# Both products of each attention score on a full 128-row operand: the low half of k stacked twice, in both layers

## The chip, the cores and the metric

The kernel runs on one core of one Trainium2 chip. The metric is device time in microseconds (us) of one execution, taken as the median of several. TensorE (PE) does the matrix products, VectorE (DVE) and ScalarE (ACT) the elementwise work, GpSimd (POOL) some elementwise work and the issue of one DMA queue, SyncE (SP) the issue of another.

## The reference

A two-layer backbone over 256 context and 512 latent tokens (768 in all, width 1024). Layer 0 mixes with differential attention beside a gated delta rule, layer 1 with a bidirectional linear recurrence (RG-LRU) beside windowed attention; a gated convolutional feed-forward follows each. The change touches only the scores of the two attentions:

```
def _diff_attend(q, k, v, lam):                 # layer 0: 4 heads, 2 maps m, 64 wide
    s = jnp.einsum('bqhmd,bkhmd->bhmqk', q, k).astype(jnp.float32) * (A_HD ** -0.5)
    p = jax.nn.softmax(s, axis=-1)
    w = p[:, :, 0] - lam * p[:, :, 1]
    return jnp.einsum('bhqk,bkhe->bqhe', w.astype(v.dtype), v)
...
    def attend(q, k, v, mask):                  # layer 1: 8 query heads on 2 k/v heads, 64 wide
        s = jnp.einsum('bqhgd,bkhd->bhgqk', q, k).astype(jnp.float32) * (D_HD ** -0.5)
        if mask is not None:
            s = jnp.where(mask, s, NEG_INF)
        p = _sink_softmax(s, sink)
        return jnp.einsum('bhgqk,bkhd->bqhgd', p.astype(v.dtype), v)
```

## The kernel before

Products that must be as good as float32 are made of a high and a low part of each operand: hi is the rounded value, lo what is left. A score is q_hi k_hi + q_lo k_hi + q_hi k_lo. Heads are 64 wide, and the operands lie with the head's 64 numbers over the partitions, so the first two terms fit into one 128-row product: one operand tile holds q_hi in one half of the 128 partitions and q_lo in the other, and the k tile holds k_hi twice. The third term is a second product with 64 rows only: the half of the q tile that holds q_hi, and the matching half of a tile with k_lo.

**Layer 0, `attn_head` (L596 on).** Heads run one after the other. For each there are three groups of query tiles of 128 queries: tiles 2 and 3 and tiles 4 and 5 against all 768 keys, tiles 0 and 1 against the 256 context keys. Per query tile and map m a score of 128 queries is written to a PSUM buffer `sc` (three buffers), in pieces of 512 and 256 key columns; each piece is the 128-row product at L613 and then the 64-row product at L614. A pair of the two stands below as "a pair": there are 20 in each head, 8 with 512 columns and 12 with 256, so 80 in all. VectorE then takes the row maximum (`reduce_max`, L615, `st`), ScalarE the exponential (L617, `e`, five buffers), VectorE normalises the two maps and subtracts them (L619 to L621), PE transposes the result (L626) and multiplies it with v (L631, `pav`). Gate projections (plain 128-row products, L341 to L344) are placed behind heads 0 and 1. The order of all instructions comes from a scheduler in the framework that builds the program, not from the code's order alone.

`attn_load` (L953 on) fetches the q and k tiles of a head from DRAM on POOL's DMA queue (L962): five tiles of tag `qk` per head by nine DMAs, four pairs of 64-row DMAs and a 128-row one (both maps' k_lo, one after the other). The tag has `NQK` = 7 buffers, so two tiles of the next head can be loaded while all five of a head are in use.

**Layer 1, `swa_block` (L1220 on).** 32 blocks (4 query tiles, 2 k/v heads, 4 query heads each): two 128-row products (L1237, the context columns and the window), two 64-row products (L1239), masks added by a bf16 product (L1242), then maximum, exponential (L1248), transposes (L1255) and the product with v (L1260). The layer's `sc` has one PSUM buffer. `halves` (L931) splits k into `k1` (k_hi in one half of the rows, copied to the other half by a POOL DMA, one tile per k/v head) and `k1l` (k_lo of head 0 in rows 0 to 63 and of head 1 in rows 64 to 127, one tile). These tiles come from a ring of `SLOTS` = 22 slots shared with the recurrence (`lt`, `gx`, `la`); `SL1` = 16 is the size of another pool, with the 16 tiles of the layer's normalised input.

Of the kernel before, what the change touches and what calls it, by code (L numbers as in the profile page):

```python
# [9 lines left out]
F32 = mybir.dt.float32  # L10
F32R = mybir.dt.float32r
BF16 = mybir.dt.bfloat16
AF = mybir.ActivationFunctionType
ALU = mybir.AluOpType
# [4 lines left out]
P = 128  # L19
# [223 lines left out]
class K:  # L243
# [213 lines left out]
        nc.vector.scalar_tensor_tensor(q, x, 0.0, q, op0=ALU.max, op1=ALU.add)  # L457
        return q

# [1 line left out]
    def ada_init(self):  # L461
        nc = self.nc
        self.sv = self.small(16, "sv")
# [79 lines left out]
            B.append(self.mod[l][s][:, 8 * m:8 * (m + 1)])  # L543
        return A, B

# [1 line left out]
    def loadx(self, pool=None, eng=None):  # L547
        xs = []
        for kt in range(KT):
# [46 lines left out]
    def attn_head(self, h, qk, Vh, o, pool, ae):  # L596
        nc = self.nc
        ident = self.c("ident")
        for (t0, nt, k1) in ((2, 2, T), (4, 2, T), (0, 2, NC)):
            nkt = k1 // P  # L600
            wts = [pool.tile([P, 3, 256], F32, tag="wT", name=self.nm("wT"), bufs=NWT) for _ in range((nkt + 2) // 3)]
            for qi in range(nt):
                qt = t0 + qi
                es = []
                st = pool.tile([P, 6], F32, tag="st", name=self.nm("st"), bufs=8)
                for m in range(2):
                    ps = self.big("sc")
                    q, k, kl = qk[3 * m], qk[3 * m + 1], qk[2]
                    lq = q[:, qt * P:qt * P + P]
                    half = slice(64 * m, 64 * m + 64)  # L610
                    for a in range(0, k1, 512):
                        b = min(a + 512, k1)
                        nc.tensor.matmul(ps[:, a:b], lq, k[:, a:b], start=True, stop=False)  # L613
                        nc.tensor.matmul(ps[:, a:b], lq[half], kl[half, a:b], start=False, stop=True)  # L614
                    nc.vector.reduce_max(st[:, m:m + 1], ps[:, 0:k1], axis=AX.X, negate=True)  # L615
                    e = ae.tile([P, T], F32, tag="e", name=self.nm("e"), bufs=NE)
                    nc.scalar.activation(e[:, 0:k1], ps[:, 0:k1], AF.Exp, bias=st[:, m:m + 1], accum_out=st[:, 2 + m:3 + m])  # L617
                    es.append(e)
                nc.vector.reciprocal(st[:, 4:6], st[:, 2:4])  # L619
                nc.vector.tensor_scalar(es[1][:, 0:k1], es[1][:, 0:k1], st[:, 5:6], self.nlam, op0=ALU.mult, op1=ALU.mult)  # L620
                nc.vector.scalar_tensor_tensor(es[0][:, 0:k1], es[0][:, 0:k1], st[:, 4:5], es[1][:, 0:k1], op0=ALU.mult, op1=ALU.add)  # L621
                for g in range(0, nkt, 3):
                    gn = min(3, nkt - g)
                    pt = self.sml("pT")
                    for j in range(gn):
                        nc.tensor.transpose(pt[:, j * P:j * P + P], es[0][:, (g + j) * P:(g + j + 1) * P], ident)  # L626
                    nc.scalar.activation(wts[g // 3][:, 0:gn, qi * P:qi * P + P],
                                         pt[:, 0:gn * P].rearrange("p (a b) -> p a b", a=gn), AF.Copy)
            po = self.sml("pav")
            for kt in range(nkt):  # L630
                nc.tensor.matmul(po[:, 0:nt * P], Vh[:, kt * P:kt * P + P], wts[kt // 3][:, kt % 3, 0:nt * P],  # L631
                                 start=kt == 0, stop=kt == nkt - 1)
            nc.scalar.activation(o[:, t0 * P:(t0 + nt) * P], po[:, 0:nt * P], AF.Copy)
# [297 lines left out]
    def halves(self, x, st, l, moves):  # L931
        nc = self.nc
        rows = (slice(0, 64), slice(64, P))
        for i, (me, other) in enumerate((rows, rows[::-1])):
            nc.scalar.activation(st[i][me], x[me], AF.Copy)
            HE[i](nc).tensor_tensor(l[me], x[me], st[i][me].bitcast(F32), op=ALU.subtract)
            dst, src = moves[i]
            HQ(nc).dma_start(dst[other], src[me])

# [13 lines left out]
    def attn_load(self, h, at):  # L953
# [1 line left out]
        up, dn = slice(0, 64), slice(64, P)  # L955
        q, k = self.qdr[h], self.qdr[4 + h]
        r = []
        for src in (((q, 0, up), (q, 1, up)), ((k, 0, up), (k, 0, up)), ((k, 1, slice(0, P)),),
                    ((q, 1, dn), (q, 0, dn)), ((k, 0, dn), (k, 0, dn))):
            t = at.tile([P, T], F32R, tag="qk", name=self.nm("qk"), bufs=NQK)  # L960
            for o, (d, i, rows) in zip((up, dn) if len(src) > 1 else (slice(0, P),), src):
                nc.gpsimd.dma_start(t[o], d[i, rows])  # L962
            r.append(t)
        return r

    def attn_v(self, h, u):
# [253 lines left out]
    def swa_block(self, i, qs, kk, V):  # L1220
# [7 lines left out]
        for kv in range(2):  # L1228
            ks = slice(64 * kv, 64 * kv + 64)
            pT = [lp.tile([P, 512], F32, tag="pT1", name=self.nm("pT1"), bufs=7) for _ in range(nkt)]  # L1230
            for g in range(4):
# [4 lines left out]
                for o, a, b in cols:  # L1236
                    nc.tensor.matmul(ps[:, o:o + b - a], lq, kst[kv][:, a:b], start=True, stop=False)  # L1237
                for o, a, b in cols:
                    nc.tensor.matmul(ps[:, o:o + b - a], lq[ks], kl[ks, a:b], start=False, stop=o == 256)  # L1239
                ms = [j for j in range(lo, hi) if j != i]  # L1240
                for j in ms:
                    nc.tensor.matmul(ps[:, 512 + (j - lo) * P:512 + (j - lo + 1) * P], self.mk[:, 0, :],  # L1242
# [29 lines left out]
    def layer1_body(self, xs, r):  # L1272
# [4 lines left out]
        with tc.tile_pool(name="l1", bufs=1, reuse_waits="tile") as lp:  # L1277
# [7 lines left out]
            kk = self.slot([P, T], F32, "kk")  # L1285
            nc.scalar.activation(kk, ps[:, 256:1024], AF.Copy)
            self.rope(kk, self.slot([P, NL], F32, "rt"), eng=RE[0] and nc.vector)
            kst, kl = [self.slot([P, T], F32R, "k1") for i in range(2)], self.slot([P, T], F32R, "k1l")
            self.halves(kk, kst, kl, [(kst[0], kst[0]), (kst[1], kst[1])])
            ps = psv  # L1290
            vT = self.slot([P, T], F32, "vT")
            nc.scalar.activation(vT, ps[:, 256:1024], AF.Copy)
# [56 lines left out]
AD1 = 7  # L1349
OH = 0  # L1350
GATES = ((0, 1), (2, 3), (), ())
NQK = 7
NE = 5
NWT = 3
ADS = 2
# [11 lines left out]
PSML = 1  # L1367
LOPOOL = 3
SFF = 7
SL1 = 16  # L1370
NY = 4
WRAW = 3
WHL = 4
# [21 lines left out]
```

## Time and profile before

| what | value |
|---|---|
| runs (us) | 2015.21, 2019.02, 2019.27; median 2019.02 |
| profiled execution | span 2016.1 us from its first to its last instruction; no other time of it is given |
| mean granted TensorE clock | 0.933 |
| PE busy | 1881.8 us, 93% of the span |
| DVE busy | 1281.7 us, 64% |
| ACT busy | 902.6 us, 45% |
| POOL busy | 498.7 us, 25% |

"Granted clock" is the share of full TensorE speed that the chip allowed: 1.00 is 2.4 GHz, 0.50 is 1.2 GHz. Layer 0's attention lies between 507 and 685 us of the span, layer 1's windowed attention between 1393 and 1572 us. In a timeline row the first number is the start, the second the time until the instruction's end; successive matmuls overlap (the next one's columns enter while the last one's results drain), so the cost of one in a row of matmuls is the distance between starts, not the second number.

### The profile page before, as it was taken

To read this page: it belongs to the slowest core of one execution; us is meant where nothing else is said; L and a number is where in the kernel's file an instruction comes from. 1 tells how busy PE (TensorE), PEld (TensorE's weight loads), DVE (VectorE), ACT (ScalarE), POOL (GpSimd) and SP (SyncE) were. 2 spreads that over 40 slices of the span, in tenths; PEclk is the share of its full clock that TensorE was granted. 3 is DMA by queue.
4 is the path that set the end of the run, shared out by engine and by line. 5 is a ranking of instruction groups with operands and counts; after the bars stand their busy time and mean duration, and the time that the engine had idled before them with its cause. 6 is when DMAs were issued, how large, how long until landed. Compare 5 with 4: busy or idle time off the path is not lost. (4 is left out here: it accounts for less than half of the span.)

```text
span 2016.1 us, 26630 instructions
## 1 busy us (share of the span) xinstructions
PE 1881.8 (93%) x9929; PEld 1509.7 (75%) x9929; DVE 1281.7 (64%) x2364; ACT 902.6 (45%) x1638; POOL 498.7 (25%) x352
## 2 busy tenths in 40 slices
PE   7687889899999999999999999979999999999997
PEld 2576778778666688888888888867555688888887
DVE  5987888775446556665755454576666685555556
ACT  4355533342556455432334232365566464333344
POOL 1546322212121024312323122132121331111112
PEclk9799988788788799999999999989999999999998
DMA  8434222222321133323344334233000232333324
GB/s 313 147 105 146 79 91 91 92 69 69 68 60 45 53 125 126 117 91 114 129 129 138 113 123 136 82 96 92 27 21 21 68 126 89 111 94 95 94 79 121
DMA packets 74801, 200.86 MB, mean 100 GB/s; under 512 B 8320, under 2 KB 18736, under 8 KB 74288
## 3 DMA queue, kind: packets, MB, share of 16 engines
q1 hardware_dynamic: 65984, 173.01, 26.6%
q10 hardware_dynamic: 4752, 16.85, 2.5%
q0 software_dynamic: 3936, 9.31, 2.2%
q8 instruction: 78, 1.28, 0.2%
q14 instruction: 51, 0.42, 0.1%
HBM read 187.71 MB, written 9.99 MB: 98 GB/s over the span
## 5 line engine op out<-in xcount | busy, mean ns | idle before, releaser
L328 ACT ACTIVATE hi<-raw 128x512 fp32r<-128x512 f32 (+2 forms) x429 | 262.0, 616 | 447.1 <-PE pj L342 197.5
L341 PE MATMUL pj<-uh,hi 128*128 128x512 f32 x1248 | 441.1, 353 | 16.1 <-DVE cv L433 13.0
L342 PE MATMUL pj<-ul,hi 128*128 128x512 f32 x1248 | 413.8, 351 | 0.0
L330 POOL TENSOR_TENSOR lo<-raw,hi 128x512 fp32r<-128x512 f32 (+1 forms) x143 | 194.2, 1358 | 791.0 <-ACT hi L328 783.2
L344 PE MATMUL pj<-uh,lo 128*128 128x512 f32 x1248 | 347.1, 353 | 0.0
L330 DVE TENSOR_TENSOR lo<-raw,hi 128x512 fp32r<-128x512 f32 (+2 forms) x286 | 207.0, 727 | 158.0 <-ACT hi L328 156.5
L341 PEld LDWEIGHTS pj<-uh,hi 128*128 128x128 f32 x1248 | 242.7, 194 | 73.1 <-issue 11.1
L342 PEld LDWEIGHTS pj<-ul,hi 128*128 128x128 f32 x1248 | 242.4, 194 | 28.7 <-issue 0.2
L344 PEld LDWEIGHTS pj<-uh,lo 128*128 128x128 f32 x1248 | 203.0, 196 | 4.4 <-issue 0.8
L433 DVE SCALAR_TENSOR_TENSOR y<-pj,smt,y 128x511 f32<-128x511 f32 (+1 forms) x264 | 161.6, 655 | 57.8 <-ACT y L423 55.2
L341 PE MATMUL dn<-h,hi 128*128 128x512 f32 (+1 forms) x560 | 194.9, 348 | 1.5 <-ACT hi L328 1.0
L342 PE MATMUL dn<-l,hi 128*128 128x512 f32 (+1 forms) x560 | 186.9, 346 | 0.0
L344 PE MATMUL dn<-h,lo 128*128 128x512 f32 (+1 forms) x560 | 169.4, 347 | 1.9 <-DVE lo L330 1.3
L558 DVE SCALAR_TENSOR_TENSOR x<-dn,mod,x 128x512 f32<-128x512 f32 (+1 forms) x152 | 93.2, 634 | 90.6 <-PE dn L344 90.4
L518 ACT ACTIVATE srow<-srow 128x1024 f32<-128x1024 f32 x56 | 59.3, 1058 | 159.9 <-POOL srow L517 159.8
L341 PE MATMUL pj<-u,hi 128*128 128x512 f32 x336 | 130.7, 389 | 0.0
L342 PE MATMUL pj<-u,hi 128*128 128x512 f32 x336 | 130.7, 389 | 0.0
L344 PE MATMUL pj<-u,lo 128*128 128x512 f32 x336 | 130.7, 389 | 0.0
L341 PEld LDWEIGHTS dn<-h,hi 128*128 128x128 f32 x560 | 106.0, 189 | 22.9 <-ACT hi L328 2.2
L517 POOL TENSOR_TENSOR srow<-ada1w,srow 128x1024 f32<-128x1024 f32 x32 | 79.6, 2487 | 173.0 <-DMA ada1w<-in_ada 128.5
L342 PEld LDWEIGHTS dn<-l,hi 128*128 128x128 f32 x560 | 106.2, 190 | 13.7 <-issue 0.5
L523 DVE SCALAR_TENSOR_TENSOR ada1w<-ada1w,srow 128x1024 f32<-128x1024 f32 x40 | 54.6, 1365 | 76.8 <-DMA ada1w<-in_ada 36.4
(394 smaller groups left out, 3406.6 us busy)
## 6 DMA issues: line engine op xcount, KB each, us to landing
raw<-in_wu SPq DMA_DIRECT2D x88, 512.0 KB, 3.5
ada1w<-in_ada SPq DMA_DIRECT2D x48, 512.0 KB, 3.6
raw<-in_w SPq DMA_DIRECT2D x38, 512.0 KB, 3.7
raw<-in_wd SPq DMA_DIRECT2D x72, 256.0 KB, 2.7
adaw<-in_ada0t ACTq DMA_DIRECT2D x24, 512.0 KB, 3.6
adaw<-in_ada SPq DMA_DIRECT2D x16, 512.0 KB, 7.4
raw<-in_w0o SPq DMA_DIRECT2D x16, 512.0 KB, 3.5
raw<-in_wd SPq DMA_DIRECT2D x40, 192.0 KB, 2.4
```

What stands on the lines that cost most here:

```text
L328: nc.scalar.activation(hi, raw[:, a:b], AF.Copy)
L330: eng.tensor_tensor(lo, raw[:, a:b], hi.bitcast(F32), op=ALU.subtract)
L341: nc.tensor.matmul(ps, hi[n], xh[:, a:b], start=n == 0, stop=False)
L342: nc.tensor.matmul(ps, hi[n], xl[:, a:b], start=False, stop=False)
L344: nc.tensor.matmul(ps, lo[n], xh[:, a:b], start=False, stop=n == last)
L433: nc.vector.scalar_tensor_tensor(y[:, o0:o1], ps[:, 256 + o0 + s:256 + o1 + s], taps[i], y[:, o0:o1], op0=ALU.mult, op1=ALU.add)
L517: nc.gpsimd.tensor_tensor(junk, raw, self.srow[:, 0, :], op=ALU.mult)
L518: nc.scalar.activation(junk, junk, AF.Copy, accum_out=col(0))
L523: nc.vector.scalar_tensor_tensor(raw, raw, 1.0, self.srow[:, i, :], op0=ALU.mult, op1=ALU.mult, accum_out=col(i))
L558: nc.vector.scalar_tensor_tensor(xs[m][:, a:b], ps[:, 256 + a:256 + b], self.mod[l][0 if a >= NC else 1][:, 8 * mi + m:8 * mi + m + 1], xs ...
```

## The change

The low half of k is stacked twice over the partitions as the high half was, so that the second product of each score also takes the full 128-row q tile. It computes (q_hi + q_lo) k_lo where q_hi k_lo was computed. In layer 0 each map gets a k_lo tile of its own: six tiles per head by twelve 64-row DMAs, and `NQK` is 8. In layer 1 there are two `k1l` tiles, each filled to 128 rows by one more POOL DMA, and `SL1` is 17. Two comments fall away, so lines 610 to 935 are one lower in the changed kernel. The numbers of matmuls, of VectorE and of ScalarE instructions do not change.

```diff
@@ -605,13 +605,12 @@
                 st = pool.tile([P, 6], F32, tag="st", name=self.nm("st"), bufs=8)
                 for m in range(2):
                     ps = self.big("sc")
-                    q, k, kl = qk[3 * m], qk[3 * m + 1], qk[2]
+                    q, k, kl = qk[3 * m:3 * m + 3]
                     lq = q[:, qt * P:qt * P + P]
-                    half = slice(64 * m, 64 * m + 64)
                     for a in range(0, k1, 512):
                         b = min(a + 512, k1)
                         nc.tensor.matmul(ps[:, a:b], lq, k[:, a:b], start=True, stop=False)
-                        nc.tensor.matmul(ps[:, a:b], lq[half], kl[half, a:b], start=False, stop=True)
+                        nc.tensor.matmul(ps[:, a:b], lq, kl[:, a:b], start=False, stop=True)
                     nc.vector.reduce_max(st[:, m:m + 1], ps[:, 0:k1], axis=AX.X, negate=True)
                     e = ae.tile([P, T], F32, tag="e", name=self.nm("e"), bufs=NE)
                     nc.scalar.activation(e[:, 0:k1], ps[:, 0:k1], AF.Exp, bias=st[:, m:m + 1], accum_out=st[:, 2 + m:3 + m])
@@ -933,7 +932,8 @@
         rows = (slice(0, 64), slice(64, P))
         for i, (me, other) in enumerate((rows, rows[::-1])):
             nc.scalar.activation(st[i][me], x[me], AF.Copy)
-            HE[i](nc).tensor_tensor(l[me], x[me], st[i][me].bitcast(F32), op=ALU.subtract)
+            lo = l[i] if isinstance(l, list) else l
+            HE[i](nc).tensor_tensor(lo[me], x[me], st[i][me].bitcast(F32), op=ALU.subtract)
             dst, src = moves[i]
             HQ(nc).dma_start(dst[other], src[me])
 
@@ -955,12 +955,12 @@
         up, dn = slice(0, 64), slice(64, P)
         q, k = self.qdr[h], self.qdr[4 + h]
         r = []
-        for src in (((q, 0, up), (q, 1, up)), ((k, 0, up), (k, 0, up)), ((k, 1, slice(0, P)),),
-                    ((q, 1, dn), (q, 0, dn)), ((k, 0, dn), (k, 0, dn))):
-            t = at.tile([P, T], F32R, tag="qk", name=self.nm("qk"), bufs=NQK)
-            for o, (d, i, rows) in zip((up, dn) if len(src) > 1 else (slice(0, P),), src):
-                nc.gpsimd.dma_start(t[o], d[i, rows])
-            r.append(t)
+        for half in (up, dn):
+            for src in (((q, 0), (q, 1)), ((k, 0), (k, 0)), ((k, 1), (k, 1))):
+                t = at.tile([P, T], F32R, tag="qk", name=self.nm("qk"), bufs=NQK)
+                for o, (d, i) in zip((up, dn), src):
+                    nc.gpsimd.dma_start(t[o], d[i, half])
+                r.append(t)
         return r
 
     def attn_v(self, h, u):
@@ -1236,7 +1236,7 @@
                 for o, a, b in cols:
                     nc.tensor.matmul(ps[:, o:o + b - a], lq, kst[kv][:, a:b], start=True, stop=False)
                 for o, a, b in cols:
-                    nc.tensor.matmul(ps[:, o:o + b - a], lq[ks], kl[ks, a:b], start=False, stop=o == 256)
+                    nc.tensor.matmul(ps[:, o:o + b - a], lq, kl[kv][:, a:b], start=False, stop=o == 256)
                 ms = [j for j in range(lo, hi) if j != i]
                 for j in ms:
                     nc.tensor.matmul(ps[:, 512 + (j - lo) * P:512 + (j - lo + 1) * P], self.mk[:, 0, :],
@@ -1285,8 +1285,10 @@
             kk = self.slot([P, T], F32, "kk")
             nc.scalar.activation(kk, ps[:, 256:1024], AF.Copy)
             self.rope(kk, self.slot([P, NL], F32, "rt"), eng=RE[0] and nc.vector)
-            kst, kl = [self.slot([P, T], F32R, "k1") for i in range(2)], self.slot([P, T], F32R, "k1l")
+            kst, kl = ([self.slot([P, T], F32R, n) for i in range(2)] for n in ("k1", "k1l"))
             self.halves(kk, kst, kl, [(kst[0], kst[0]), (kst[1], kst[1])])
+            for i, (me, other) in enumerate(((slice(0, 64), slice(64, P)), (slice(64, P), slice(0, 64)))):
+                HQ(nc).dma_start(kl[i][other], kl[i][me])
             ps = psv
             vT = self.slot([P, T], F32, "vT")
             nc.scalar.activation(vT, ps[:, 256:1024], AF.Copy)
@@ -1349,7 +1351,7 @@
 AD1 = 7
 OH = 0
 GATES = ((0, 1), (2, 3), (), ())
-NQK = 7
+NQK = 8
 NE = 5
 NWT = 3
 ADS = 2
@@ -1367,7 +1369,7 @@
 PSML = 1
 LOPOOL = 3
 SFF = 7
-SL1 = 16
+SL1 = 17
 NY = 4
 WRAW = 3
 WHL = 4
```

On PE the instructions stand in the same order but for a few places. One is the start of the fourth head's scores. In the names, `sc_` is the score's PSUM buffer, the first `qk` the k tile, the second the q tile. Before (L613 the 128-row, L614 the 64-row product; `qk_793` to `qk_795` are map 0's, `qk_796` and `qk_797` with `qk_795` are map 1's):

```order
L613 MATMUL sc_804_5131<-qk_797_5116,qk_796_5113 128x512
L614 MATMUL sc_804_5131<-qk_795_5111,qk_796_5113 128x512
L613 MATMUL sc_804_5131<-qk_797_5116,qk_796_5113 128x256
L614 MATMUL sc_804_5131<-qk_795_5111,qk_796_5113 128x256
L613 MATMUL sc_809_5153<-qk_794_5108,qk_793_5105 128x512
L614 MATMUL sc_809_5153<-qk_795_5111,qk_793_5105 128x512
L613 MATMUL sc_809_5153<-qk_794_5108,qk_793_5105 128x256
L614 MATMUL sc_809_5153<-qk_795_5111,qk_793_5105 128x256
```

The scores are computed one after the other: map 1 of the first query tile, then map 0 of the second. In the changed kernel (L612 the first, L613 the second product; `qk_796` to `qk_798` are map 0's, `qk_799` to `qk_801` map 1's):

```order
L612 MATMUL sc_808_5147<-qk_800_5129,qk_799_5126 128x512
L612 MATMUL sc_813_5169<-qk_797_5120,qk_796_5117 128x512
L613 MATMUL sc_813_5169<-qk_798_5123,qk_796_5117 128x512
L612 MATMUL sc_813_5169<-qk_797_5120,qk_796_5117 128x256
L613 MATMUL sc_813_5169<-qk_798_5123,qk_796_5117 128x256
L612 MATMUL sc_815_5177<-qk_800_5129,qk_799_5126 128x512
L613 MATMUL sc_808_5147<-qk_801_5132,qk_799_5126 128x512
L612 MATMUL sc_808_5147<-qk_800_5129,qk_799_5126 128x256
L613 MATMUL sc_808_5147<-qk_801_5132,qk_799_5126 128x256
```

The second product of map 1 (`qk_801` is the last tile loaded) has moved behind map 0 of the second query tile and behind the first product of that tile's map 1.

On POOL, the loads of head 0 (`qdr` is the DRAM copy of q and k), followed by the first of head 1. Before:

```order
L962 DMA qk_576_4172<-qdr_113 64x768 x2
L962 DMA qk_577_4175<-qdr_113 64x768 x2
L962 DMA qk_578_4178<-qdr_113 128x768
L962 DMA qk_579_4180<-qdr_113 64x768 x2
L962 DMA qk_580_4183<-qdr_113 64x768 x2
L962 DMA qk_654_4536<-qdr_113 64x768 x2
```

After:

```order
L962 DMA qk_576_4172<-qdr_113 64x768 x2
L962 DMA qk_577_4175<-qdr_113 64x768 x2
L962 DMA qk_578_4178<-qdr_113 64x768 x2
L962 DMA qk_579_4181<-qdr_113 64x768 x2
L962 DMA qk_580_4184<-qdr_113 64x768 x2
L962 DMA qk_581_4187<-qdr_113 64x768 x2
L962 DMA qk_655_4540<-qdr_113 64x768 x2
```

The 128-row load of both maps' k_lo is gone; each map has a k_lo tile of two 64-row DMAs, map 0's third and map 1's sixth of the head.

## Rows read from the trace of the kernel before

**Rows 1.** The page's first part, TensorE: busy us, share of the span, instructions.

```profile
PE 1881.8 (93%) x9929; PEld 1509.7 (75%) x9929; DVE 1281.7 (64%) x2364; ACT 902.6 (45%) x1638; POOL 498.7 (25%) x352
```

**Rows 2.** The waits: engine, line, releaser; us in total, times, longest us.

```profile
DVE st L615 <- PE sc L614: 32.9, 30, 3.2
...
PEld sc L1237 <- ACT e L1248: 13.7, 14, 3.6
```

**Rows 3.** PE's timeline in a score burst at full clock: start, us to end.

```profile
653.14 0.38 PE L614 MATMUL sc<-qk,qk 64*128 64x256 f32 x1
653.45 0.50 PE L613 MATMUL sc<-qk,qk 128*128 128x512 f32 x1
653.89 0.49 PE L614 MATMUL sc<-qk,qk 64*128 64x512 f32 x1
654.31 0.38 PE L613 MATMUL sc<-qk,qk 128*128 128x256 f32 x1
```

**Rows 4.** PE's timeline in a projection with 128 rows throughout, at full clock.

```profile
605.12 0.39 PE L342 MATMUL pj<-ul,hi 128*128 128x512 f32 x1
605.34 0.28 PE L341 MATMUL pj<-uh,hi 128*128 128x256 f32 x1
605.46 0.28 PE L342 MATMUL pj<-ul,hi 128*128 128x256 f32 x1
```

**Rows 5.** PE's timeline in the same score burst, later, at half clock.

```profile
659.52 0.79 PE L613 MATMUL sc<-qk,qk 128*128 128x512 f32 x1
660.24 0.79 PE L614 MATMUL sc<-qk,qk 64*128 64x512 f32 x1
660.96 0.58 PE L613 MATMUL sc<-qk,qk 128*128 128x256 f32 x1
661.48 0.58 PE L614 MATMUL sc<-qk,qk 64*128 64x256 f32 x1
```

**Rows 6.** PE's timeline in a projection with 128 rows throughout, at half clock.

```profile
1358.77 0.63 PE L355 MATMUL pj<-ul,hi 128*128 128x512 f32 x1
1359.19 0.63 PE L353 MATMUL pj<-uh,hi 128*128 128x512 f32 x1
```

**Rows 7.** The windows, instructions of L613 alone: PE busy (count), PEld, PEclk, DMA share, GB/s.

```profile
508.70:532.60 23.90, 10.85 (x17) 4.69 (x16) 0.50 0.04 11
570.10:587.20 17.10, 8.02 (x12) 3.49 (x12) 0.50 0.08 29
624.70:641.80 17.10, 6.62 (x10) 2.97 (x10) 0.50 0.00 0
655.40:675.90 20.50, 7.23 (x12) 3.25 (x11) 0.50 0.00 0
```

**Rows 8.** DVE's timeline in the fourth head's score burst.

```profile
650.98 0.96 DVE L615 TENSOR_REDUCE st<-sc 128x1 f32<-128x768 f32 x1 [1.11 <-PE sc L614]
...
660.50 0.67 DVE L620 TENSOR_SCALAR e<-e,st,nlam 128x768 f32<-128x768 f32 x1
...
662.97 1.01 DVE L621 SCALAR_TENSOR_TENSOR e<-e,st,e 128x768 f32<-128x768 f32 x1
...
667.02 0.96 DVE L615 TENSOR_REDUCE st<-sc 128x1 f32<-128x768 f32 x1 [0.51 <-PE sc L614]
```

**Rows 9.** PE's timeline in a score block of layer 1.

```profile
1393.11 0.40 PE L1237 MATMUL sc<-k,q 128*128 128x256 f32 x2
...
1393.87 0.23 PE L1242 MATMUL sc<-mk 128*128 128x128 bf16 x1
```

**Rows 10.** The windows, rest of heads 1 and 3 behind their score bursts.

```profile
584.00:599.00 15.00, 14.98 (x74) 12.14 (x74) 7.68 (x16) 8.87 (x24) 4.72 (x9) 0.89 0.52 111
666.90:684.90 18.00, 17.98 (x74) 14.17 (x74) 7.67 (x16) 8.89 (x24) 0.00 (x0) 0.75 0.00 0
```

**Rows 11.** POOL's timeline before the fourth head.

```profile
644.35 2.67 POOL L962 DMA_DIRECT2D qk<-qdr  x5 [25.37 <-PE sc L613]
```

**Rows 12.** The DMAs: queue, kind, count, KB each, us from issue to landing.

```profile
qk<-qdr POOLq DMA_DIRECT2D x32, 192.0 KB, 5.1
```

## The prediction

> **What bounds the kernel now.** The page first: PE is busy for 93% of the span [rows 1], so a gain has to come out of PE's time or out of the few places where PE waits. The waits come second. In the attention of layer 0 the engine that waits is not PE but DVE: its row maxima wait 32.9 us for the second product of the score, L614 [rows 2]. Within a head's burst of scores, then, PE is the bound and DVE follows close behind it. The timeline of PE in such a burst is the view that decides. The reader is to compare distances between starts. At full clock a 128-row product of 512 columns starts at 653.45, the 64-row one on the same columns at 653.89, the next 128-row one at 654.31: 0.44 and 0.42 us. Behind a 64-row product of 256 columns the next start comes 0.31 us later [rows 3]. In a projection, where every product has 128 rows, the same column counts cost 0.22 and 0.12 us [rows 4]. The added 0.2 us does not depend on the column count and comes at both changes, 128 to 64 rows and back: a change of the row count keeps the next product from starting while the last one is still under way. At half clock the distances are 0.72 us (512 columns) and 0.52 us (256) [rows 5] against 0.42 us for 512 columns in a projection at the same clock [rows 6], so about 0.21 us for 256 by halving: 0.30 us added each time.
>
> **What is removed: the switches.** The changed kernel has the same matmuls with the same columns, and all of a score's are 128 rows high. What I assume is that they then cost what a projection's cost. A pair (both products of one piece) then gains, warm, 0.86 - 0.44 = 0.42 us for 512 columns and 2 x 0.31 - 0.24 = 0.38 us for 256; as 256 columns are the more frequent, 0.39 us. Cold it gains 1.44 - 0.85 = 0.59 us and 2 x 0.52 - 0.43 = 0.61 us; 0.59 us. How many are cold: the four stretches at a granted clock of 0.50 hold 17, 12, 10 and 12 of the 80 first products, 51 in all [rows 7]. One at an edge counts only in part, so I take 50 cold and 30 warm. PE's time falls by 50 x 0.59 + 30 x 0.39 = 29.5 + 11.7 = 41.2 us in layer 0.
>
> Not all of that becomes span, since DVE is next in line. In the fourth head the first of eight large maxima starts at 650.98 and the eighth at 667.02, 16.0 us apart [rows 8]. DVE's own work between is seven maxima of 0.96, two L620 of 0.67 and two L621 of 1.01 us [rows 8], 10.1 us. If PE is no longer late, this stretch can shrink by 5.9 us at most; I take 5.5 for the small reciprocals between. PE alone needs, for the seven scores (each 512 + 256 columns twice), 7 x 2 x 0.34 = 4.8 us warm or 7 x 2 x 0.63 = 8.8 us cold, below 10.1 either way, so DVE becomes the bound of the burst. The six pairs of this head that lie behind the eighth maximum's score are the context group's and the last large one's; they lie among transposes and `pav` products where PE has other work, and I credit them with about 0.3 us each, 1.9 us. So the head gains 7.4 us of the 12 x 0.59 + 8 x 0.39 = 10.2 us that PE saves in it, 0.73. This share on all four heads gives 41.2 x 0.73 = 30 us. From another side, the whole of DVE's 32.9 us of waiting [rows 2] is about as much as the bursts have to give, which agrees.
>
> **What is removed in layer 1.** A block starts at 1393.11 and its mask product at 1393.87 [rows 9]: 0.76 us for four products of 256 columns that cost 4 x 0.12 = 0.48 us in a projection. 0.28 us for each of 32 blocks makes 9.0 us. The blocks lie between projections, so PE can use what is freed, save where a block waits for the single score buffer (13.7 us of waiting for the exponential, [rows 2]); there a shorter score only lengthens the wait. The ring of slots loses one slot to the second k_lo tile, and the recurrence's tiles wait for a somewhat later release. I take 2 us off for both: 7 us, with 0 and 9 as the bounds.
>
> **What is added.** Layer 0: each head's loads become twelve DMAs of 64 rows instead of eight and one of 128. POOL issues one in 2.67 / 5 = 0.53 us [rows 11], and such a pair of DMAs lands 5.1 us after issue [rows 12], so the three more add 1.6 us to the issue and map 1's k_lo tile, now the last, arrives so much later. For heads 1 and 2 gate projections lie between the release of the tiles and the first score, and for head 0 the loads are issued long before; those arrivals are hidden as long as these projections last. Only before the fourth head is there no such cover; the first five DMAs are issued from 644.35 on, released by the third head's last score [rows 11]. As the first section's order rows show, the scheduler puts map 1's second product behind the next tile's map 0, which gives the late tile some 1.3 us of PE's time. On PE, everything behind that product waits with it: the next score, then its maximum on DVE. Bounds: nothing, if the tiles arrive in time, to 1.6 us plus a k_lo tile of map 0 that lands in 5 us instead of less; I take 1.5 us in all. Layer 1: two more POOL DMAs of 64 rows, 1.1 us of issue, 5 us to land, issued together with the k tiles; the first score is at 1393.11, behind the q projections, which hide them. Uncovered they would cost at most 6 us, once. The added term q_lo k_lo costs no column. The weight of the second product is now loaded with 128 rows; weight loads lie beside the matmul before them, so I price that at nothing; the bound from above is that of the third rival.
>
> **The sum.** 30 - 1.5 + 7 = 35.5 us. The profiled execution's span is 2016.1 us, so 1980.6 us. The median of the runs, 2019.0 us, lies 2.9 us above this span: 1983 us.
>
> **Rivals.** First, the clock gives part of it back. All four stretches at 0.50 begin while scores run [rows 7]. If DVE orders the burst, PE works it in shorter spells with waits between, and a granted clock that stays at 0.50 further into the head costs: what is left of a head behind its burst takes 15.0 us at a mean of 0.89 and 18.0 us at 0.75, with 74 matmuls in both [rows 10], so 3 us per head. One lasting step of this size in all four heads is 12 us, which leaves a gain of 23 us: 1996 us. For it speaks that the bursts are where the clock falls, against it that it falls there already while PE shows no gaps. The Trainium skill ("TensorE: Matmul & The Clock Gate", section "A second HAM failure mode: psum-queue depth-cycling") says that a kernel whose PE idles briefly between groups of matmuls while it cycles through PSUM buffers goes back and forth between the two clocks; by this rule the first rival is what happens here. The trace agrees only in that the low clock sits in the bursts; gaps of PE are not needed for it there.
>
> Second, more than I forecast: the clock stays high. The cold stretches are 78.6 us long and hold 32.7 us of first products [rows 7]; second products about as many, so some 13 us are transposes and `pav` products at half speed. If half of the stretches went, about 10 us would come on top, and with the full 9 us of layer 1 the gain is 48 us: 1971 us; beyond 1966 only if PE's 41.2 us came whole as well.
>
> Third, on the other side: a 64-row product might be nearly free where two lie in different halves of the array or beside a 128-row one, and what the rows show as 0.2 us of switching might be the product's own time in another guise. Then a full-row second product costs its whole time in addition: with 50 of 80 cold, 32 of 512 columns and 48 of 256, 20 x 0.42 + 12 x 0.22 + 30 x 0.21 + 18 x 0.12 = 19.5 us, and 64 x 0.12 = 7.7 us in layer 1, 27 us more: 2046 us. It decides from the point at which a 64-row product takes less than its plain time. Against it stands every distance in [rows 3] and [rows 5], none of which lies below 0.31 us. The Trainium skill ("TensorE: Matmul & The Clock Gate", part 3 on packing small matmuls) says that products in different row groups of the array run at the same time, which speaks against this change; here no such overlap is seen, each 64-row product delays the next start.
>
> Fourth, nothing happens: the 0.2 us may come from accumulating into the same PSUM columns, not from the rows. Against this: in a projection two products into the same columns follow at 0.12 us [rows 4], and the next piece, which has other columns, waits 0.42 us all the same [rows 3]. It would give 2019 us.
>
> **Chances and range.** Forecast as worked out (gain 24 to 50 us) 0.78; first rival (15 to 24 us) 0.09; second, beyond 53 us, 0.05; fourth, with late loads eating a small rest, 0.04; third 0.04. This kernel's measurement can tell a change from none at about 0.2%, 4 us. Faster is forecast plus first and second rival, with a little of the fourth: 0.93; same 0.03; slower 0.04. The range: the term of layer 0 lies between 41.2 x 0.45 = 18.5 us (the clock loses what rival one says) and 43 us, layer 1 between 0 and 9 us. That gives gains of 20 to 53 us, 1966 to 1999 us.
>
> **What would show it.** Right: starts of a score's products 0.22 to 0.24 us (512) and 0.12 us (256) apart at full clock, or 0.42 and 0.21 us at half; DVE's wait for the score's second product down from 32.9 us to below 10 us, and PE waiting in the bursts for the exponential instead; a burst of the fourth head of about 10.5 us between first and eighth maximum; block starts in layer 1 0.48 us before their mask. Wrong: distances above 0.3 us between full-row products; a mean granted clock well below 0.933 with longer stretches behind the bursts; POOL's loads as the releaser of the first scores in more than one head, at over 9 us a head, which alone would turn the sign.

## The result

The changed kernel takes 1980.43 us (median of 4 runs, 1978.31 to 1983.4) against 2018.65 us before (median of 4). The ratio on record is 0.983, 95% interval 0.981 to 0.985, which is 35 us (31 to 39); the two medians alone are 38 us apart, a ratio of 0.981. The forecast was 1983 us, 1966 to 1999 us. The profiled execution took 1980.38 us with a span of 1978.6 us, so the span fell by 37.5 us; its time lies 1.8 us above its span, where the prediction put 2.9 us between the two.

Where that came from is shown by the windows of the two kernels, in each layer from the attention's first score to its last product with v. Before, and then in the changed kernel (length of the window; busy us and instructions of PE, PEld, DVE, ACT, POOL; granted clock; DMA):

```profile
507.59:685.04 177.45, 171.48 (x612) 114.71 (x611) 93.74 (x153) 93.38 (x184) 23.76 (x30) 0.78 0.18 44
1393.11:1572.28 179.17, 164.71 (x732) 103.53 (x730) 112.29 (x211) 108.84 (x282) 34.88 (x25) 0.96 0.10 29
```

```profile
508.05:655.77 147.72, 126.45 (x612) 101.73 (x610) 91.70 (x153) 92.16 (x184) 28.23 (x39) 0.91 0.30 65
1361.17:1534.75 173.58, 156.94 (x730) 104.06 (x728) 111.84 (x211) 107.85 (x281) 34.48 (x25) 0.95 0.10 28
```

Layer 0's attention is 29.7 us shorter and layer 1's 5.6 us. The remaining 2 us lie outside the change: matched instruction by instruction, the changed kernel reaches the first score 0.5 us later and gains 2.7 us between the two windows, most of it around 702 and 1360 us of the trace before, where matmuls that ran at half clock now run at full. In layer 0 PE has the same 612 matmuls and is busy 45.0 us less; but it also stands idle for 21.3 us of the window where it was 6.0 us. So 45 us were freed and 15 us of them came back as waiting. The waits of the changed kernel name what for (engine, line, releaser; us in total, times, longest):

```profile
PEld sc L612 <- ACT e L616: 15.8, 13, 4.4
...
PE sc L612 <- ACT e L616: 13.0, 11, 4.2
...
DVE st L614 <- PE sc L613: 10.5, 11, 2.4
```

DVE's wait for the second product fell from 32.9 us [rows 2] to 10.5 us, just short of the "below 10" that the prediction asked for. In its place PE waits 13.0 us for an exponential (L616), that is, for one of the three score buffers to come free. PE's own timeline in the fourth head's burst, first at full clock, then at half:

```profile
633.47 0.39 PE L613 MATMUL sc<-qk,qk 128*128 128x512 f32 x1
633.70 0.28 PE L612 MATMUL sc<-qk,qk 128*128 128x256 f32 x1
633.82 0.28 PE L613 MATMUL sc<-qk,qk 128*128 128x256 f32 x1
633.93 0.39 PE L612 MATMUL sc<-qk,qk 128*128 128x512 f32 x1
...
638.22 0.63 PE L612 MATMUL sc<-qk,qk 128*128 128x512 f32 x1
638.65 0.63 PE L613 MATMUL sc<-qk,qk 128*128 128x512 f32 x1
639.08 0.41 PE L612 MATMUL sc<-qk,qk 128*128 128x256 f32 x1
639.29 0.41 PE L613 MATMUL sc<-qk,qk 128*128 128x256 f32 x1
```

The starts are 0.23 us (512 columns) and 0.12 and 0.11 us (256) apart at full clock, 0.43 and 0.21 us at half. These are a projection's distances [rows 4, 6]; the 0.2 and 0.3 us on top [rows 3, 5] are gone.

What the 0.2 us were can be seen in the weight loads (PEld), one for each product. Before, at the place of [rows 3], and then in the changed kernel:

```profile
653.89 0.18 PEld L614 LDWEIGHTS sc<-qk,qk 64*128 64x128 f32 x1 [0.25 <-issue]
654.31 0.19 PEld L613 LDWEIGHTS sc<-qk,qk 128*128 128x128 f32 x1 [0.24 <-issue]
```

```profile
633.47 0.19 PEld L612 LDWEIGHTS sc<-qk,qk 128*128 128x128 f32 x1
633.70 0.19 PEld L613 LDWEIGHTS sc<-qk,qk 128*128 128x128 f32 x1
```

Before, the load starts when its own product is recorded to start (653.89, 654.31 [rows 3]): it did not run under the product before, and its 0.18 to 0.19 us come on top of the columns' 0.24 us. That holds, within 2 ns, for 138 of the 139 score products of this attention that follow a matmul with another number of rows; at half clock the load takes 0.28 to 0.29 us, the 0.3 us of [rows 5]. In the changed kernel the load for the product at 633.70 starts at 633.47 and the one for the product at 633.82 at 633.70, each with the product before it. So a change of the row count costs a weight load that is not hidden. Why the load is held back no run here shows.

What I did not expect is the clock. The mean over the attention rose from 0.78 to 0.91. In place of four long stretches at 0.50, 78.6 us in all [rows 7], there are six short ones, 24.2 us in the windows below and some 27 us by the mean clock (columns as in the windows above):

```profile
514.50:517.50 3.00, 3.00 (x11) 2.51 (x10) 2.43 (x5) 2.29 (x6) 0.00 (x0) 0.50 0.00 0
559.00:562.00 3.00, 2.71 (x9) 2.36 (x10) 1.97 (x3) 1.36 (x5) 1.82 (x1) 0.50 0.51 175
569.30:572.40 3.10, 3.10 (x12) 2.83 (x12) 2.79 (x6) 2.28 (x6) 0.00 (x0) 0.50 0.02 5
606.40:616.00 9.60, 6.69 (x20) 5.42 (x21) 6.75 (x10) 8.56 (x15) 0.00 (x0) 0.51 0.00 0
620.70:623.00 2.30, 2.30 (x7) 1.85 (x6) 2.30 (x6) 1.66 (x6) 0.00 (x0) 0.50 0.00 0
637.30:640.50 3.20, 3.20 (x11) 2.67 (x11) 2.63 (x5) 2.44 (x6) 0.00 (x0) 0.51 0.01 3
sum 24.20, PE 21.00 PEld 17.64 DVE 18.87 ACT 18.59 POOL 1.82; mean PE 3.50 PEld 2.94 DVE 3.15 ACT 3.10 POOL 0.30
```

In layer 1 a block's four products now start 0.47 us ahead of its mask (1361.17 to 1361.64) where it was 0.76 us [rows 9]:

```profile
1361.17 0.40 PE L1237 MATMUL sc<-k,q 128*128 128x256 f32 x2
1361.40 0.40 PE L1239 MATMUL sc<-k1l,q 128*128 128x256 f32 x2
1361.64 0.23 PE L1242 MATMUL sc<-mk 128*128 128x128 bf16 x1
```

### The profile page after: what moved, and what is told of

It reads as the page before. It is cut to its first block, busy times and chain, and to the rows that moved or that the text cites. A ratio compares the mean times of both kernels' runs of the same rounds, so it can differ in the third digit from the quotient of the medians.

```text
span 1978.6 us, 26655 instructions
## 1 busy us (share of the span) xinstructions
PE 1825.8 (92%) x9929; PEld 1492.9 (75%) x9929; DVE 1279.3 (65%) x2364; ACT 901.0 (46%) x1638; POOL 505.4 (26%) x366
## 3 DMA queue, kind: packets, MB, share of 16 engines
q0 software_dynamic: 4800, 11.28, 2.8%
## 5 line engine op out<-in xcount | busy, mean ns | idle before, releaser
L341 PEld LDWEIGHTS dn<-h,hi 128*128 128x128 f32 x560 | 105.7, 189 | 24.2 <-ACT hi L328 3.7
L342 PEld LDWEIGHTS dn<-l,hi 128*128 128x128 f32 x560 | 105.8, 189 | 13.7 <-issue 0.5
```

What stands on the lines that cost most here:

```text
L341: nc.tensor.matmul(ps, hi[n], xh[:, a:b], start=n == 0, stop=False)
L342: nc.tensor.matmul(ps, hi[n], xl[:, a:b], start=False, stop=False)
```

## The experiments

All ratios are to the kernel before, whose runs beside them had medians of 2015.6 us (`e1` to `e8`) and 2018.1 us (`e9` to `e11`); the changed kernel stands at 0.983 (0.981 to 0.985). A thousandth is 2 us. Three groups of runs follow: whether it is the change of the row count and nothing that came with it, what orders the bursts afterwards, and the loads.

**Each layer alone.** `e1_layer0` keeps layer 1 as before, `e2_layer1` keeps layer 0.

> Only layer 0 is changed (six q and k tiles per head, 128-row second product); layer 1 is as before. Theory (each change of the row count holds the next product back, in both layers, and the two layers add): the gain of the trace in layer 0 alone, some 30 us, so 1987 to 1991 us against 2018.7 before. Rival (the recurrence's slots and layer 1's clock are what moved, or the layers don't add): 1982 or less, or above 1994.

> Only layer 1 is changed (two k_lo tiles of 128 rows, two more copies, 128-row second product); layer 0 is as before. Theory: 5 to 7 us off, 2011.5 to 2014 us. Rival (what the trace shows there is the clock, not the switch): within 2 us of before, 2017 to 2021.

Measured: 0.9837 (0.9819 to 0.9855) and 0.9974 (0.9960 to 0.9988), 33 us and 5 us off, medians 1981.26 and 2010.35 us. The two add to 38 us, the change gives 35 (0.0174 of 2018.65, 31 to 39), or 38 by the medians. Layer 0's share came out 3 us above what was expected of it: carried to 2018.7 us the ratio is 1986 us (1982 to 1989), 1 us below the theory's range and not yet in the rival's, so the time alone does not decide. The trace does: with layer 0 alone changed, its attention takes 146.2 us, and layer 1's takes 179.1 us as before. So the layers add within the noise, and nearly all is in layer 0.

**Everything but the row count (`e3_loads_old_products`).**

```diff
-                        nc.tensor.matmul(ps[:, a:b], lq, kl[:, a:b], start=False, stop=True)
+                        nc.tensor.matmul(ps[:, a:b], lq[half], kl[half, a:b], start=False, stop=True)
```

and `lq[ks], kl[kv][ks, a:b]` in layer 1. In layer 0's map 1 these 64 rows of the q tile hold q_lo, so its score leaves out q_hi k_lo; the run is for the time alone.

> The changed kernel with all its tiles, loads, copies and its order of instructions, but the second product takes 64 rows again, in both layers. Theory (only the row count of the second product matters, and the added loads are hidden): 2017 to 2021 us, and 0.31 us between starts behind 256 columns at full clock. Rival (the gain is from the new order or the deeper buffers of q and k tiles): 1980 to 1990 us.

Measured: 0.9998 (0.9984 to 1.0012), 2015.83 us. PE's timeline at the start of its first head:

```profile
509.36 0.47 PE L613 MATMUL sc<-qk,qk 128*128 128x512 f32 x1
509.76 0.49 PE L614 MATMUL sc<-qk,qk 64*128 64x512 f32 x1
510.18 0.38 PE L613 MATMUL sc<-qk,qk 128*128 128x256 f32 x1
510.50 0.58 PE L614 MATMUL sc<-qk,qk 64*128 64x256 f32 x1
```

0.40, 0.42 and 0.32 us apart: the old distances are back, although every tile, every load and the order of instructions on PE, DVE and ACT are the changed kernel's (a few 32-row matmuls before the attention apart). With 64-row products the added loads and the new order cost and give nothing that can be measured; the row count of the second product carries the whole gain.

**64 rows, but no change of rows (`e4_both_64`).**

```diff
-                        nc.tensor.matmul(ps[:, a:b], lq, k[:, a:b], start=True, stop=False)
+                        nc.tensor.matmul(ps[:, a:b], lq[half], k[half, a:b], start=True, stop=False)
```

> The kernel before, but in layer 0 the first product takes 64 rows as well, the same half of the partitions as the second (q_lo k_hi is left out of the score). Tiles, loads and order are as before. Theory (it is the change of the row count that costs, not the 64 rows): 0.12 us between starts behind 256 columns inside a score, and 1986 to 1993 us. Rival (a 64-row product is slow by itself): 0.31 us behind all 256-column products, 2017 to 2030 us.

Measured: 0.9879 (0.9863 to 0.9894), 1991.24 us. It tells two things apart. 64 rows are not slow by themselves: most of the gain is there with no product of a score above 64 rows. And the timeline shows something else (the count behind x says how many matmuls a row stands for):

```profile
633.09 0.51 PE L613 MATMUL sc<-qk,qk 64*128 64x512 f32 x2
633.43 0.40 PE L614 MATMUL sc<-qk,qk 64*128 64x512 f32 x2
633.67 0.28 PE L613 MATMUL sc<-qk,qk 64*128 64x256 f32 x2
633.79 0.28 PE L614 MATMUL sc<-qk,qk 64*128 64x256 f32 x2
633.94 0.50 PE L613 MATMUL sc<-qk,qk 64*128 64x512 f32 x1
634.28 0.39 PE L614 MATMUL sc<-qk,qk 64*128 64x512 f32 x1
634.52 0.27 PE L613 MATMUL sc<-qk,qk 64*128 64x256 f32 x1
634.63 0.27 PE L614 MATMUL sc<-qk,qk 64*128 64x256 f32 x1
```

The last three rows are one score by itself: 0.24 us behind 512 columns and 0.11 us behind 256, as with full rows. In the rows before, two products of 512 columns of two scores, by the order of the fourth head's scores one of each map and so on different halves of the partitions, take 0.24 us together (633.43 to 633.67), the time of one. Here it is that 64-row products run side by side. The gain is still 0.4% smaller than that of `e1_layer0`, which changes layer 0 alone as well: its attention takes 154.6 us at a mean clock of 0.80, against 146.2 us at 0.92. The steps between the maps' halves and to the 128-row transposes remain, but how much each of them costs was not measured.

**Half the changes (`e5_batched`).** All 128-row pieces of a score first, then its 64-row pieces.

```diff
                         nc.tensor.matmul(ps[:, a:b], lq, k[:, a:b], start=True, stop=False)
+                    for a in range(0, k1, 512):
+                        b = min(a + 512, k1)
                         nc.tensor.matmul(ps[:, a:b], lq[half], kl[half, a:b], start=False, stop=True)
```

> The kernel before, but in layer 0 the two 128-row products of a score (512 and 256 columns) come first and then its two 64-row products. Each of the 32 large scores changes the row count twice where it did four times. Theory (the change of the row count costs): 64 of 160 changes fall away at 0.2 to 0.3 us, 16 us of PE's time, of which some 0.73 becomes span: 12 us off, ratio to before 0.994, and the first 64-row product of a score still starts late. Rival (the wait is for the product before into the same PSUM columns): none is left in these scores, 20 us off or more, ratio 0.990 or less.

Measured: 0.9933 (0.9912 to 0.9954), 13.5 us off where 12 were expected, which is in part chance: the estimate took the clock as it was, but the mean clock in its attention rose from 0.78 to 0.85. The timeline in its fourth head (L613 the 128-row, L616 the 64-row products, each time 512 and 256 columns):

```profile
641.96 0.61 PE L616 MATMUL sc<-qk,qk 64*128 64x512 f32 x2
642.50 0.62 PE L613 MATMUL sc<-qk,qk 128*128 128x512 f32 x2
643.04 0.61 PE L616 MATMUL sc<-qk,qk 64*128 64x512 f32 x2
643.59 0.62 PE L613 MATMUL sc<-qk,qk 128*128 128x512 f32 x2
```

768 columns take 0.54 to 0.55 us, which is 0.34 us for the columns and 0.20 us for one change. If the wait came from the product before into the same PSUM columns, it would be gone here, since another piece lies between. That was the fourth rival; it is out.

**What orders the bursts afterwards.** `e6_max256` relieves DVE in the changed kernel, `e7_scale_on_act` moves work from DVE to ACT.

```diff
-                    nc.vector.reduce_max(st[:, m:m + 1], ps[:, 0:k1], axis=AX.X, negate=True)
+                    nc.vector.reduce_max(st[:, m:m + 1], ps[:, 0:256], axis=AX.X, negate=True)
```

> The changed kernel, but layer 0's row maxima are taken over the first 256 columns of each score only (512 columns are left out of the maximum), which takes 32 x 0.53 = 17 us from DVE and none from PE. Theory (behind the change, DVE's maximum and the exponential behind it order the bursts): 5 to 10 us below the changed kernel, ratio to before 0.978 to 0.980. Rival (PE still orders them): within 2 us of the changed kernel, ratio 0.982 to 0.984.

Measured: 0.9771 (0.9745 to 0.9797), 11 us below the changed kernel's ratio, a little more than the 5 to 10 that were expected, with not one column less on PE. PE's wait for the exponential falls:

```profile
PE sc L612 <- ACT e L616: 7.7, 7, 4.2
```

from 13.0 to 7.7 us, and the attention of layer 0 is 134.9 us long instead of 147.7 (columns as in the windows above):

```profile
509.98:644.88 134.90, 118.22 (x609) 95.29 (x608) 76.73 (x153) 90.98 (x184) 28.31 (x39) 0.96 0.31 70
```

So behind the change the path runs through the maximum. But only 4.6 us of these 12.8 are idle time of PE that fell away; the other 8.2 are PE's busy time, shorter at a mean clock of 0.96 instead of 0.91.

```diff
-                nc.vector.tensor_scalar(es[1][:, 0:k1], es[1][:, 0:k1], st[:, 5:6], self.nlam, op0=ALU.mult, op1=ALU.mult)
+                nc.vector.tensor_tensor(st[:, 5:6], st[:, 5:6], self.nlam, op=ALU.mult)
+                nc.scalar.activation(es[1][:, 0:k1], es[1][:, 0:k1], AF.Copy, scale=st[:, 5:6])
```

> The changed kernel with the scaling of map 1 (L619) on ACT instead of DVE: 14 us less on DVE, some 18 us more on ACT, which also makes the exponentials. Theory (the chain maximum, exponential, release of the score buffer orders the bursts): DVE's relief and ACT's burden nearly cancel, 0 to 5 us below the changed kernel, ratio 0.980 to 0.983. Rival (DVE's sum alone orders them): 7 us below or more, ratio 0.979 or less.

Measured: 0.9862 (0.9838 to 0.9886), above both expectations: 7 us over the changed kernel's ratio, with intervals that still overlap. In its trace the attention of layer 0 takes 150.7 us, 3 us more, at the same mean clock. 14 us less on DVE gained nothing. In its waits:

```profile
PEld sc L612 <- ACT e L616: 20.5, 18, 4.4
...
DVE e L621 <- ACT e L620: 6.3, 12, 1.1
```

PE's weight loads wait 20.5 us for an exponential where it was 15.8, since ACT now has 0.94 us of scaling among the exponentials that release the score buffers, and DVE waits 6.3 us for the scaled tile. Read together, it is the chain from maximum to exponential to a free buffer that counts, not the sum of DVE's work. That "DVE alone" is the next bound, as the prediction had it, is too simple.

**The loads.** One DMA per tile (`e8_one_dma`). The source of a q tile is two pieces of 64 rows, that of a k tile one piece of 64 rows read twice:

```diff
-                for o, (d, i) in zip((up, dn), src):
-                    nc.gpsimd.dma_start(t[o], d[i, half])
+                (d, i), (_, j) = src
+                s = d[i:j + 1, half] if i < j else d[i:i + 1, half].to_broadcast([2, 64, T])
+                nc.gpsimd.dma_start(t[:, :], s)
```

> The changed kernel with each q or k tile of layer 0 fetched by one DMA of 128 rows instead of two of 64: six DMAs a head instead of twelve, some 3 us of POOL's issue less per head. Theory (only the fourth head's first scores wait for loads, by a fraction of what they cost): 0 to 2 us below the changed kernel, ratio 0.981 to 0.983. Rival (late loads are what keeps the gain at 35 us): 5 us below or more, ratio 0.980 or less.

Measured: 0.9895 (0.9871 to 0.9919), 14 us slower than the changed kernel, against both expectations. The DMAs of this run, then of the changed kernel, then the 128-row DMAs of the kernel before (count, KB each, us from issue to landing):

```profile
qk<-qdr POOLq DMA_DIRECT2D x24, 384.0 KB, 13.7
```

```profile
qk<-qdr POOLq DMA_DIRECT2D x48, 192.0 KB, 5.0
```

```profile
qk<-qdr POOLq DMA_DIRECT2D x4, 384.0 KB, 3.7
```

The same 384 KB land in 3.7 us from a plain source and in 13.7 us, the median over both kinds, from the sources here. The queue's packets rise from the changed kernel's 4800 to 25920 while its bytes go from 11.28 to 11.36 MB: the data's packets stayed the same, and what was added are packets of 4 bytes. Why they come, and whether it is they that take the time, was not tried. PE then waits for loads (6.9 us once, 8.0 us in three waits) at the start of the first and the fourth head, and the attention of layer 0 is 159.8 us long, 12.1 us more, of which 9.7 are idle time of PE. What was meant to test late loads by making them earlier tests them by making them later: 8.7 us more of landing time cost 14 us.

`e9_nqk12` tests it the other way: 12 buffers for q and k tiles.

> The changed kernel with 12 instead of 8 buffers for q and k tiles, so that all six tiles of a head can be loaded while the head before computes. Theory (the run with one DMA per tile was slower because those DMAs took 13.7 us to land, and in the changed kernel only the fourth head's first scores wait, by 1 to 2 us): 1 to 3 us below the changed kernel, ratio to before 0.981 to 0.982. Rival (loads cost several us in the changed kernel too): 5 us below or more, ratio 0.980 or less.

Measured: 0.9797 (0.9775 to 0.9819), 1976.01 us. The ratio itself, 6 us below the changed kernel's, lies in the rival's range, but its interval reaches into both ranges and overlaps that of the changed kernel, so the time does not decide. The attention of layer 0 is 145.6 us long, 2.1 us less: counted from the first score, the second head starts 3.8 us later, PE waiting 4.0 us more in the first, and from there on 5.9 us are gained, at a mean clock of 0.93 instead of 0.91. The 2.1 us are of the size that was expected; how much of the 6 us is real, and how much of it is the loads, stays open.

`e10_gates` and `e11_nqk12_gates` move a gate projection to the place where PE waits.

```diff
-GATES = ((0, 1), (2, 3), (), ())
+GATES = ((0, 1), (2,), (3,), ())
```

> The changed kernel with the fourth gate projection behind head 2 instead of head 1. In the changed kernel PE waits 4.3 us at the third head's start for DVE's read of a gate projection (L1060), and has nothing to do at the fourth head's start until its k tiles land. Theory (PE's waits in the bursts are where the rest of the gain went): 2 to 6 us below the changed kernel, ratio 0.9795 to 0.9815. Rival (these waits only move): within 2 us, ratio 0.982 to 0.984.

> Both: 12 buffers and the fourth gate projection behind head 2. Theory: the two overlap, since the projection also hides the loads: no more than 1 us below the gate projection's run. Rival (they are separate waits): the two gains add.

Measured: 0.9836 (0.9815 to 0.9858) and 0.9825 (0.9798 to 0.9852), neither below the changed kernel, so the rival of the first held. Counted from the first score, the third head of `e10_gates` starts 10 us earlier than in the changed kernel's trace, but the fourth 5 us later; PE's wait for DVE's read of a gate projection is 6.7 us instead of 4.3:

```profile
PE sc L612 <- DVE gt L1060: 6.7, 2, 4.3
```

The wait goes with the projection. Together with 12 buffers the gain of those is not seen either: 2 us below `e10_gates`, within the noise, so that run does not decide between its two expectations.

## Why the prediction was right

**The switch.** That a change between 128 and 64 rows costs 0.2 us at full and 0.3 us at half clock, and that full-row products cost a projection's time, held wherever full-row products of a score follow each other in the changed kernel's trace, and `e3_loads_old_products`, `e4_both_64` and `e5_batched` show it from three sides. The prediction set the weight load of the second product at nothing, since loads lie beside the matmul before them. Behind a change of the row count they do not: this load, left uncovered before and covered after, is the very 0.2 us. Summed over the two traces, from each score product's start to the next start (waits left out), layer 0's score products took 81.3 us before and 41.6 us after: 39.7 us against the 41.2 us of the sum. That they are so close is in part chance. At the distances of equal rows the same products would have taken 39.9 us at the clock that each had before, so the switches were worth 41.4 us, as forecast; the warmer clock should have taken off another 7.0 us; and 8.7 us were lost at products next to a wait or to another kind of matmul, where the short distances do not hold.

**What becomes span.** The sum gave 28.5 us for layer 0 and the windows give 29.7. The two are near each other for partly wrong reasons. I took the clock as it was, with 50 of the pairs cold before and after. In fact the cold stretches shrank to a third, so PE's transposes and products with v were shortened too and 45 us were freed instead of 41. What came back as waiting was 15 us where the share of 0.73 allowed for 11. That share was worked out on the fourth head and put on all four; from first score to first score (for the fourth to the last product with v) the heads got 10.7, 6.6, 2.4 and 9.9 us shorter. The burst of the fourth head shows the waiting. DVE's timeline there:

```profile
631.06 0.96 DVE L614 TENSOR_REDUCE st<-sc 128x1 f32<-128x768 f32 x1 [0.34 <-PE sc L613]
634.13 2.69 DVE L614 TENSOR_REDUCE st<-sc 128x1 f32<-128x768 f32 x3 [2.11 <-PE sc L613]
...
643.65 0.94 DVE L614 TENSOR_REDUCE st<-sc 128x1 f32<-128x768 f32 x1
```

From the first to the eighth maximum it takes 12.6 us, not 10.5, so it shrank by 3.4 us and not by 5.5: 2.1 us of it is the wait before the second maximum. (The two large pairs outside this stretch are those of the first score, ahead of the first maximum, and not of the last one, as the prediction has it; its 1.9 us stay the same.) PE's first scores there wait for a tile:

```profile
632.93 0.70 PE L612 MATMUL sc<-qk,qk 128*128 128x512 f32 x2 [0.41 <-DMA qk<-qdr]
```

That was the place that I gave; the wait is 0.41 us, where I took 1.5 us for late loads in all. How much of the rest of the 2.1 us is the later tile and how much the order of the products was not tried. The further step "DVE becomes the bound of the burst" was short of a link: PE waits for the exponential that frees a score buffer, and `e6_max256` with `e7_scale_on_act` puts the path through maximum and exponential together.

**Layer 1.** 9.0 us by the distances and 7 us after deductions; the windows give 5.6, and the time of `e2_layer1` 5 (2 to 8). The two terms of the sum held: the blocks' score products took 30.4 us before and 21.2 us after, 9.2 us less, and PE's idle time in the window rose from 14.5 to 16.6 us. The waits of the blocks for the exponential did not shrink (PEld's was 13.7 us [rows 2], after it is 14.2). In the trace of `e2_layer1` the same stretch, at the clock of before, takes 172.5 us, 6.7 us less:

```profile
1385.31:1557.82 172.51, 155.69 (x730) 102.79 (x728) 111.82 (x211) 108.02 (x281) 34.53 (x25) 0.96 0.09 28
```

So 7 us was right at an unchanged clock, and in the changed kernel's trace the mean clock of 0.95 instead of 0.96 goes with the missing 1 us. How much of the added idle time is the score buffer and how much the ring was not tried.

**The rivals.** The first, a clock that stays low longer, is refuted in its sign: the trace has 15 us more of PE's gaps in the attention and a granted clock of 0.91 instead of 0.78. By the rule of the Trainium skill ("TensorE: Matmul & The Clock Gate", section "A second HAM failure mode: psum-queue depth-cycling") the clock goes back and forth when PE idles between groups. It does so here, six times, but four times before as well, when PE idled for 6.0 us in all, and the sum of the low stretches fell from 78.6 us to 24.2. The second rival's mechanism happened, a warmer clock, and about as much as it freed came back as waiting at the score buffers. I had no price for that pairing; that the two nearly offset each other is luck. The third, products of 64 rows side by side, is not in the kernel before, but `e4_both_64` shows that the mechanism exists, as the Trainium skill says ("TensorE: Matmul & The Clock Gate", part 3 on packing small matmuls). There two 64-row products of two scores stood next to each other; in layer 0 of the kernel before each one had 128-row products on both sides. The fourth is out by `e5_batched`.

## What to carry to other kernels

Look at the distance between starts of matmuls, not at their busy time, wherever the number of rows alternates: in this kernel each change cost 0.2 us at full clock, as much as 512 columns, for a weight load that was no longer hidden, and filling up the smaller operand, even with a term that isn't needed, cost PE no time. After such a gain, look for the next link in the buffer chain (here maximum, exponential, free score buffer) before more is taken from PE, and don't expect it on one engine. A second way of writing the same load is not the same load: a DMA's landing time is to be read from the trace before the loads around it are called hidden.

## What was not expected of the hardware

With more idle time of PE the granted clock was higher: 78.6 us at 0.50 before, 24.2 us after, at 612 matmuls both times. The two do not simply go together: in the attention of layer 0 PE idled 15.6 us in `e4_both_64` at a mean clock of 0.80, 16.7 us in `e6_max256` at 0.96 and 25.9 us in `e11_nqk12_gates` at 0.86. What sets the clock here stays open. The weight load of a product that follows one with another number of rows did not start while that one ran. Two 64-row products of 512 columns on different halves of the partitions took 0.24 us together. A DMA of 128 rows whose source is two pieces of 64, or one read twice, landed in 13.7 us on POOL's queue, one of the same 384 KB from a plain source in 3.7 us.
